# Weights of the projections stored in 4 KB rows, and the one-hots of the gates' second index built on VectorE

## The chip, the core and the metric

One of the eight cores of a Trainium2 chip runs the whole layer; the other cores take no part. The core has TensorE (PE, with its weight loads shown apart as PEld), VectorE (DVE), ScalarE (ACT), GpSimd (POOL) and SyncE (SP), each with a queue of instructions that it takes in order, and 16 DMA engines that all queues share. The metric is the device time of one execution in microseconds, and a measurement of this kernel can tell about 1% from no change.

## The reference, cut to what matters

```python
proj = einsum('bsd,de->bse', rms_norm(x, norm_mix), w_in)      # 1024 tokens, 1024 -> 2560 channels
o_sb = stick_breaking_attention(q, k, v)                        # 8 heads of 64
o_rg = rg_lru(conv(x_rg)) * gelu(g_rg)                          # 512 channels
x = x + concat(rms_norm(o_sb), rms_norm(o_rg)) @ w_out          # 1024 -> 1024
h = rms_norm(x)
# PEER: 8 heads, two halves of 128 keys each, 16384 experts of one neuron
q = einsum('td,dhk->thk', h, w_query)                           # 1024 -> 2048
s = einsum('thpk,hpnk->thpn', q, sub_keys)
top 16 of each half; top 16 of their 256 sums: idx = i1 * 128 + i2, g = softmax
act = gelu(einsum('td,thkd->thk', h, expert_u[idx]))            # 128 slots for each token
x = x + einsum('thk,thkd->td', g * act, expert_v[idx])
```

All arithmetic is float32, and the two expert tables have 64 MB each.

## The kernel before

The 1024 tokens are 8 tiles of 128. They go through the first half of the layer in five groups: tile 0, tiles 1 and 2, 3 and 4, 5 and 6, and 7. Each group has stages with one letter each: n (norm), i (projections to q, k, v), p and r (the RG-LRU branch), a (attention), o (output projection), q (PEER queries, scores, and the 16 best of each half) and s (the 16 best pairs, their experts and softmax). The weights come in pieces of 512 KB, each 128 columns of a matrix: `columns` loads them for w_in (`wi`, `wx`, `wg`) and w_q (`wq`), and `out_proj` loads `wo`. In memory the matrices lie as in the reference, so that a piece of 128 columns is 1024 runs of 512 bytes (2 KB for `wo`). Four buffers hold `wi`, `wx` and `wg`, three hold `wo` and `wq`.

The expert part is done in two ways. Tiles 0, 1, 2 and 7 are **gathered**: for each of their 4 x 128 = 512 slots, POOL issues an indirect DMA that fetches 128 rows of expert_u (512 KB, one row for each token) and later one of expert_v. DVE takes the dot product with `h2` (`u`, line 663) and adds the weighted rows into `y` (line 678). Tiles 3 to 6 are **dense**: for every block e of 128 experts, all 512 tokens are multiplied with the block's expert_u (`s`), passed through gelu (`ga`), weighted with the gate of each token and expert, and multiplied with the block's expert_v (`acc`, `rot`). The products are float32 in three passes of split operands (`uh`, `ul`, `vh`, `vl`, `wh`, `wl`).

The gates of a dense tile come from `gates`. Expert i1 * 128 + i2 has its gate at row i2, column i1 of a 128 x 128 matrix for each token, which is a product over the 128 slots of two matrices: `oa`, the one-hots of i1, and `ob`, the one-hots of i2 times the gate. Four tokens make a group, and a tile has 32 groups, so there are 128 in all. For `ob`, PE first writes i2 - i for every slot, token and column i into PSUM: `less` (line 602) multiplies the transposed i2 with a widened identity, and line 603 adds -i. DVE then compares with zero and multiplies with the gate in one instruction (line 620). `oa` is made on ACT (lines 608 and 609) or on DVE (line 611), by the table `OZS`. PE multiplies `ob` and `oa` into `pg` (line 623), ACT copies that to `gs` (line 624), and a DMA writes each block of 32 tokens to `gd` in DRAM. The dense experts read `gd` back as `gt`, four expert blocks at a time, and line 719 multiplies `ga` with it: the first `ga` can start only when all gates have been written.

The order of the instructions on each queue is not that of the code. `ORDER` gives each stage a priority, and the framework sets the order of every queue when the program is built, from its own model of how long things take:

```python
with tile.TileContext(nc, schedule_with_timeline_sim=True) as tc:
```

Two constants set how the gathered slots are spread. The first `FREE` = 27 blocks of 8 slots (216 slots) may go ahead of the dense experts. Each of the other 296 slots waits for its turn, which is a value that ACT copies from the weights `wh` of a dense block (line 726), so that they keep step with the 128 blocks:

```python
if (k * P + PH) // n_turn == e:
    nc.scalar.activation(turn[:, k:k + 1], wh[:, 0:1].bitcast(F32), AF.Copy)
```

So the program has a mixed part up to the first `ga`, a dense part of 128 blocks in which gathers run beside the products, and an end in which the last gathered slots and the additions of the outputs remain. What is called a slot done below is one `y` instruction on DVE.

Of the kernel before, what the change touches and what calls it, by code (L numbers as in the profile page):

```python
# [46 lines left out]
# the order of priority of the stages of the groups, of the gates of a tile (g), of blocks of gathers (x)  # L47
# [10 lines left out]
def layer(ctx, tc, x, w_in, w_out, w_q, vecs, rga, rgx, skT, eu, ev, euT, out,  # L58
# [14 lines left out]
    # the banks that the last stages do not use are apart: the dense experts start in them  # L73
# [8 lines left out]
    # gate matrices of the dense tokens: gd[j, block of TB tokens, i, token], for expert i * 128 + j  # L82
# [36 lines left out]
    # means over 512 channels, over the channels of a head  # L119
# [6 lines left out]
    # heads 2 c and 2 c + 1 of 8 to chunk c of channels  # L126
# [10 lines left out]
    nob = cp.tile([1, P], BF16, name="nob")  # L137
    nc.vector.tensor_scalar(nob, ioi[0:1, :], -1.0, None, op0=OP.mult)
    ones_b = cp.tile([1, P], BF16, name="ones_b")
    nc.vector.memset(ones_b, 1.0)  # L140
    # rank16[k, s] = k
# [6 lines left out]
    # softplus(-lam) = max(-lam, 0) + ln(1 + exp(-|lam|))  # L148
# [21 lines left out]
    def mm(dst, a, b, first=True, last=True):  # L170
        """dst += sum over k of a[k].T @ b[k]: float32, or pairs of float32r parts"""
# [13 lines left out]
    def columns(pool, tag, w, c0, name, bufs):  # L185
# [10 lines left out]
    def rstd_of(dst, mean):  # L196
        """1 / sqrt(mean + eps)"""
# [25 lines left out]
    # sums of pairs in rows of 8: what no pair takes stays out of reach  # L223
# [3 lines left out]
    # the sums and the normalised rows of the gathered tiles  # L227
# [3 lines left out]
    def norm_in(g):  # L231
# [7 lines left out]
        # x -> h^T  # L239
# [5 lines left out]
    def in_proj(g):  # L245
# [6 lines left out]
        # q, k, v; q stays without its rstd, which the scores take  # L252
        rqk = keep.tile([P, 3, n, 8], F32, tag="rq", name="rq", bufs=2)
        G[g]["rq"] = rqk[:, 1:3]
        for dst, c1, gain, nm in ((kT[:, :, t0:t0 + T], 4, 1, "pk"), (qT, 0, 0, "pq")):
            for c in range(4):
                raw = columns(pj, "wraw", w_in, (c1 + c) * P, "wi", WI)
# [22 lines left out]
        for c in range(4):  # L280
            raw = columns(pj, "wraw", w_in, 1024 + c * P, "wi", WI)
# [6 lines left out]
    def rg_proj(g):  # L288
        """channels on partitions"""
# [4 lines left out]
        for e in range(4):  # L294
            wx = columns(pj, "wraw", w_in, 1536 + e * P, "wx", WI)
            wg = columns(pj, "wraw", w_in, 2048 + e * P, "wg", WI)
# [15 lines left out]
    def rg_lru(g):  # L312
# [16 lines left out]
        # 1 - a^2 = (1 + a^2) tanh(-log a)  # L329
# [9 lines left out]
        # the rstd of each token, to all channels  # L339
# [16 lines left out]
    def attention(g):  # L356
        act, qT, rq = (G[g][nm] for nm in ("act", "qT", "rq"))
        for i, tl in enumerate(groups[g]):
# [3 lines left out]
            # heads that share a bank of scores, from one half of the partitions  # L362
            hp = max(1, 512 // N)
            for h0 in {1: range(8), 2: (0, 1, 4, 5), 4: (0, 1)}[hp]:
                po = bank("po", "po", 1)
                right = None
                for c0 in range((N - 1) // 512 * 512, -1, -512):
# [17 lines left out]
                    for s in range(hp):  # L385
                        # om[k] = product of om from k on; the last position of all is masked in every row
# [7 lines left out]
                    if c0:  # L394
                        # the product over this whole chunk
# [17 lines left out]
    def out_proj(g):  # L413
# [35 lines left out]
    def queries(g, heads=range(8)):  # L449
        """PEER queries, scores, the 16 best of each half"""  # L450
# [392 lines left out]
```

## Time and profile before

| what | value |
| --- | --- |
| median of 3 runs | 2909.61 us |
| lowest and highest | 2885.03 and 2914.87 us |
| span of the profiled execution | 2904.6 us (its own time beside the span is not listed) |
| busy share of the span | PE 92%, DVE 83%, ACT 46%, POOL 48% |
| DMA | 888.90 MB, 306 GB/s over the span |

The profile shows one execution. The span is the time from its first to its last instruction; the median of the runs lies 5.0 us above it. The busy time of an engine is the sum of its instructions, and matmuls are pipelined, so that PE counts as busy a little longer than it is. A granted clock of 1.00 is TensorE's full 2.4 GHz.

### The profile page before, as it was taken

What the parts mean: (1) busy time and instruction counts of PE and PEld (TensorE: products, weight loads), DVE (VectorE), ACT (ScalarE), POOL (GpSimd) and SP (SyncE); (2) the same over time, 40 slices, a digit from 0 to 9 for tenths busy, and PEclk for the clock granted to TensorE, in tenths of its full rate; (3) what the DMA queues carried; (4) which work ended last, traced back from release to release, by engine and by line L of the source; (5) the groups of instructions that cost most, each with busy time, mean ns of one, the idle gap of its engine ahead of it and who ended that gap; (6) DMA issues with size and microseconds to landing.
All of it is one profiled execution on the core that took longest, in us unless ns stands there. A gap on an engine that the chain in (4) does not pass through costs nothing.

```text
span 2904.6 us, 38604 instructions
## 1 busy us (share of the span) xinstructions
PE 2659.0 (92%) x12664; PEld 2103.5 (72%) x12664; DVE 2404.2 (83%) x5235; ACT 1336.3 (46%) x3255; POOL 1401.6 (48%) x1110
## 2 busy tenths in 40 slices
PE   7896989888997988988789999999999999999994
PEld 7685757766784576666567888888888888888883
DVE  2168779987998879998879979888888889888898
ACT  4426434434355633986834443434444434444432
POOL 0134654354444443323446546555655556555565
PEclk9997999898997889978889999999999999999997
DMA  8596888899977688987999989999999999999998
GB/s 235 162 325 223 289 308 297 268 308 297 293 237 250 226 288 291 327 285 268 334 321 360 347 315 365 328 338 352 323 347 339 333 325 352 334 348 329 335 331 307
DMA packets 470168, 888.90 MB, mean 306 GB/s; under 512 B 27600, under 2 KB 286672, under 8 KB 467920
## 3 DMA queue, kind: packets, MB, share of 16 engines
q0 software_dynamic: 147456, 536.94, 52.2%
q1 hardware_dynamic: 322512, 349.51, 36.1%
q8 instruction: 100, 1.64, 0.2%
q14 instruction: 100, 0.82, 0.1%
HBM read 841.25 MB, written 45.09 MB: 305 GB/s over the span
## 4 chain that ended last, share of the span: by engine, by line
PE 61%; DMA 13%; DVE 11%; issue 6%; ACT 5%; POOL 3%; SPq 0%; POOLq 0%; DVEq 0%; ACTq 0%
PE s L177 23%; PE acc L177 16%; PE rot L177 5%; DMA v<-in_ev_dram,idx 4%; DMA u<-in_eu_dram,idx 3%; DMA wq<-in_w_q_dram 3%; PE pqq L194 2%; PE pg L623 2%; DVE u L663 2%; PE pxg L194 2%; DVE y L678 2%; PE pv L285 2%; PE po L429 1%; PE z L377 1%; POOL v L652 1%
## 5 line engine op out<-in xcount | busy, mean ns | idle before, releaser
L652 POOL DMA_INDIRECT u<-in_eu_dram,idx x512 | 666.7, 1302 | 702.0 <-DVE y L678 340.5
L652 POOL DMA_INDIRECT v<-in_ev_dram,idx x512 | 665.2, 1299 | 609.7 <-DVE y L678 193.0
L678 DVE SCALAR_TENSOR_TENSOR y<-v,dots,y 128x1024 f32<-128x1024 f32 x512 | 654.9, 1279 | 48.4 <-DMA v<-in_ev_dram,idx 43.4
L663 DVE SCALAR_TENSOR_TENSOR u<-u,h 128x1024 f32<-128x1024 f32 x512 | 617.3, 1218 | 63.3 <-DMA u<-in_eu_dram,idx 62.0
L177 PE MATMUL s<-h2T,uh 128*128 128x512 f32 x2048 | 505.2, 396 | 0.0
L177 PEld LDWEIGHTS s<-h2T,uh 128*128 128x128 f32 x2048 | 385.5, 188 | 93.4 <-issue 0.2
L177 PE MATMUL acc<-vh,wl 128*128 128x512 f32 x768 | 300.1, 391 | 21.3 <-DVE wl L183 21.2
L177 PE MATMUL acc<-vl,wh 128*128 128x512 f32 x768 | 300.5, 391 | 0.1
L177 PE MATMUL acc<-vh,wh 128*128 128x512 f32 x768 | 299.9, 391 | 0.0
L177 PE MATMUL s<-h2T,ul 128*128 128x512 f32 x1024 | 264.3, 398 | 2.0 <-DVE ul L183 2.0
L194 PE MATMUL pqq<-act,wq 128*128 128x256 f32 (+1 forms) x1280 | 243.1, 347 | 10.9 <-DMA wq<-in_w_q_dram 10.9
L194 PEld LDWEIGHTS pqq<-act,wq 128*128 128x128 f32 x1280 | 208.7, 196 | 36.1 <-DMA wq<-in_w_q_dram 13.1
L177 PEld LDWEIGHTS s<-h2T,ul 128*128 128x128 f32 x1024 | 193.2, 189 | 49.3 <-DVE ul L183 1.8
L182 ACT ACTIVATE vh<-vr 128x512 fp32r<-128x512 f32 x256 | 159.1, 627 | 149.1 <-PE acc L177 70.1
L183 DVE TENSOR_TENSOR vl<-vr,vh 128x512 fp32r<-128x512 f32 x256 | 174.4, 687 | 50.6 <-ACT vh L182 47.1
L623 PE MATMUL pg<-oa,ob 128*128 128x128 f32 x1024 | 166.1, 315 | 37.8 <-DVE ob L620 26.6
L623 PEld LDWEIGHTS pg<-oa,ob 128*128 128x128 f32 x1024 | 148.2, 221 | 64.4 <-issue 22.4
L177 PEld LDWEIGHTS acc<-vh,wl 128*128 128x128 f32 x768 | 144.8, 189 | 53.6 <-issue 21.0
L717 ACT ACTIVATE ga<-s 128x512 f32<-128x512 f32 x128 | 76.4, 597 | 222.9 <-PE s L177 221.3
L624 ACT ACTIVATE gs<-pg 128x512 f32<-128x512 f32 x128 | 136.2, 1080 | 86.2 <-PE pg L623 69.4
L183 DVE TENSOR_TENSOR ul<-ur,uh 128x1024 fp32r<-128x1024 f32 x128 | 156.4, 1222 | 14.3 <-ACT uh L182 13.5
L177 PEld LDWEIGHTS acc<-vl,wh 128*128 128x128 f32 x768 | 144.9, 189 | 31.8 <-DVE vl L183 0.5
(238 smaller groups left out, 4445.1 us busy)
## 6 DMA issues: line engine op xcount, KB each, us to landing
vr<-in_ev_dram SPq DMA_DIRECT2D x128, 512.0 KB
ur<-in_euT_dram SPq DMA_DIRECT2D x128, 512.0 KB
wq<-in_w_q_dram SPq DMA_DIRECT2D x80, 512.0 KB
gd<-gs SPq DMA_DIRECT2D x16, 2048.0 KB
gt<-gd SPq DMA_DIRECT2D x32, 1024.0 KB
wi<-in_w_in_dram SPq DMA_DIRECT2D x60, 512.0 KB
wo<-in_w_out_dram SPq DMA_DIRECT2D x40, 512.0 KB
wx<-in_w_in_dram SPq DMA_DIRECT2D x20, 512.0 KB
```

The source lines that it names most:

```text
L177: nc.tensor.matmul(dst, a[k][u], b[k][v], start=first and i == 0, stop=last and i == len(terms) * n - 1)
L182: nc.scalar.activation(hi, src, AF.Copy)
L183: nc.vector.tensor_tensor(lo, src, hi.bitcast(F32), op=OP.subtract)
L194: nc.tensor.matmul(dst, w[:, k, :], act[:, k, :], start=k == 0, stop=k == DK - 1)
L285: nc.tensor.matmul(pv[:, i * P:(i + 1) * P], act[:, k, i * P:(i + 1) * P], raw[:, k, :], start=k == 0, stop=k == DK - 1)
L377: nc.tensor.matmul(zz, qT[pp, h // 2, qs], kT[pp, h // 2, c0:c0 + w], start=True, stop=not diag)
L623: nc.tensor.matmul(pg[:, t * P:(t + 1) * P], ob[:, t, :], oa[:, t, :], start=True, stop=True)
L624: nc.scalar.activation(gs[:, :, t4:t4 + 4].rearrange("p i t -> p t i"), pg.rearrange("p (t i) -> p t i", t=4), AF.Copy)
L652: nc.gpsimd.indirect_dma_start(out=t, out_offset=None, in_=table, in_offset=bass.IndirectOffsetOnAxis(ap=idx[:, s:s + 1], axis=0))
L663: nc.vector.scalar_tensor_tensor(u, u, 1.0, h2, op0=OP.mult, op1=OP.mult, accum_out=dots[:, s:s + 1])
L678: nc.vector.scalar_tensor_tensor(y, v, dots[:, s:s + 1], y, op0=OP.mult, op1=OP.add)
L717: nc.scalar.activation(ga, sp[:, :ND], AF.Gelu_apprx_tanh)
```

## The change

The host stores w_in and w_q as pieces of 128 columns, [piece, partition, chunk, column], and w_out as pieces [half, quarter, partition, chunk, column], so that each partition's share of a piece is one run of 4 KB. The sub-keys are stored by head, their runs of 1 KB stay. The buffers, the sizes of the pieces and their number are as before.

In `gates`, i1 and i2 are both transposed into `tr`, and `less` and its constants go: 256 matmuls on PE with their weight loads, and the 128 instructions of line 620, give way to 512 `tensor_scalar` instructions on DVE, one for each token. Each compares the row 0 to 127 (`iof`) with the token's i2 and multiplies with its gate, both given as one value for each partition. `tr` gets a second buffer.

```diff
     def columns(pool, tag, w, c, name, bufs):
         raw = pool.tile([P, DK, P], F32, tag=tag, name=name, bufs=bufs)
-        nc.sync.dma_start(raw, w[:, c0:c0 + P].rearrange("(k p) n -> p k n", p=P))
+        nc.sync.dma_start(raw, w[c])
         return raw
...
-                nc.sync.dma_start(raw, w_out[q * 256:(q + 1) * 256, c * 512:(c + 1) * 512].rearrange("(k p) n -> p k n", p=P))
+                nc.sync.dma_start(raw, w_out[c, q])
...
-        tr = gp.tile([P, 3, P], F32, tag="tr", name="tr", bufs=1)
+        tr = gp.tile([P, 3, P], F32, tag="tr", name="tr", bufs=2)
         pb = bank("in", "pb", 2, BF16)
-        nc.tensor.transpose(pb[:, 0:P], i1, ident_b)
-        nc.scalar.activation(tr[:, 0], pb[:, 0:P], AF.Copy)
+        for s in range(2):
+            nc.tensor.transpose(pb[:, s * P:(s + 1) * P], ij[:, s].rearrange("p h k -> p (h k)"), ident_b)
+        nc.scalar.activation(tr[:, 0:2], pb[:, 0:2 * P].rearrange("p (s t) -> p s t", s=2), AF.Copy)
         pt = b_in("pt")
         nc.tensor.transpose(pt[:, 0:P], gtl.rearrange("p h k -> p (h k)"), ident)
-        nc.scalar.activation(tr[:, 1], pt[:, 0:P], AF.Copy)
-        nc.scalar.activation(tr[:, 2], pt[:, 0:P], AF.Copy, scale=-1.0)
+        nc.scalar.activation(tr[:, 2], pt[:, 0:P], AF.Copy)
...
-                def less(ix):
-                    """index - i, for every i, for the slots of 4 tokens"""
-                    d = bank("in" if i < GS else "z", "d", 2).rearrange("p (t i) -> p t i", t=4)
-                    nc.tensor.matmul(d, ix, ident_b[:, tk:tk + 4, None].to_broadcast(sh), start=True, stop=False)
-                    nc.tensor.matmul(d, ones_b, nob[:, None, :].to_broadcast([1, 4, P]), start=False, stop=True)
-                    return d
...
-                    nc.vector.scalar_tensor_tensor(ob, less(i2), 0.0, tr[:, 1, tk:tk + 4, None].to_broadcast(sh), op0=OP.is_equal, op1=OP.mult)
+                for t in range(4):
+                    nc.vector.tensor_scalar(ob[:, t], iof, tr[:, 1, tk + t:tk + t + 1], tr[:, 2, tk + t:tk + t + 1], op0=OP.is_equal, op1=OP.mult)
```

Since the framework orders the queues anew, the change also moves instructions. Up to the first gates the order is the same on every engine. Three places of the new order follow; a row is one instruction, with xN for N equal ones in a row, and the line numbers are those of each kernel.

On PE, in the gates of tiles 5 and 6, before: each group of four tokens has its two difference products and their weight loads ahead of the four products `pg`.

```order
L602 LDWEIGHTS ij
L602 MATMUL d<-ident_b,ij 128x512
L603 LDWEIGHTS ones_b
L603 MATMUL d<-nob,ones_b 128x512
L623 MATMUL pg<-oa,ob 128x128 x4
L602 LDWEIGHTS ij
L602 MATMUL d<-ident_b,ij 128x512
L603 LDWEIGHTS ones_b
L603 MATMUL d<-nob,ones_b 128x512
L623 MATMUL pg<-oa,ob 128x128 x8
```

The same place on PE in the changed kernel: the queries `pqq` and scores `sc` of tile 7 are all ahead, and the 128 products of tile 5 and those of tile 6 stand alone.

```order
L189 MATMUL pqq<-act,wq 128x128 x16
L465 MATMUL sc<-skh,qq 128x128 x2
L580 LDWEIGHTS ij
L580 MATMUL pb<-ident_b,ij 128x128
L603 MATMUL pg<-oa,ob 128x128 x128
L580 LDWEIGHTS ij
L580 MATMUL pb<-ident_b,ij 128x128
L583 MATMUL pt<-ident,g 128x128
L172 MATMUL s<-h2T_9750,ul 128x512 x8
```

On DVE, ahead of the first `ga` of the dense experts, before: the last `ob` of the gates is four rows and six slots away from it (`u` and `y` are gathered slots, `vl` a split of expert_v).

```order
L620 SCALAR_TENSOR_TENSOR ob<-d,tr 128x512
L678 SCALAR_TENSOR_TENSOR y<-v,dots,y 128x1024 x4
L183 TENSOR_TENSOR vl<-vr,vh 128x512 x2
L678 SCALAR_TENSOR_TENSOR y<-v,dots,y 128x1024
L183 TENSOR_TENSOR vl<-vr,vh 128x512 x2
L678 SCALAR_TENSOR_TENSOR y<-v,dots,y 128x1024
L663 SCALAR_TENSOR_TENSOR u,dots<-u,h_20539 128x1024 x2
L719 TENSOR_TENSOR ga<-ga,gt 128x512 x2
```

The same place on DVE in the changed kernel: the end of the selection for tile 7 (`oh`, `ijw`, `idx`) now lies there too. Counted over the whole queue, 184 slots are done ahead of the first `ga`, where it was 208, and 473 ahead of the last one, where it was 498.

```order
L658 SCALAR_TENSOR_TENSOR y<-v,dots,y 128x1024
L545 TENSOR_TENSOR oh<-oh 128x4x32
L658 SCALAR_TENSOR_TENSOR y<-v,dots,y 128x1024
L546 TENSOR_TENSOR ijw<-oh 128x64
L643 SCALAR_TENSOR_TENSOR u,dots<-u,h_20535 128x1024
L554 SCALAR_TENSOR_TENSOR idx<-ijw 128x128
L643 SCALAR_TENSOR_TENSOR u,dots<-u,h_20535 128x1024
L178 TENSOR_TENSOR vl<-vr,vh 128x512 x2
L643 SCALAR_TENSOR_TENSOR u,dots<-u,h_20535 128x1024
L178 TENSOR_TENSOR vl<-vr,vh 128x512 x2
L643 SCALAR_TENSOR_TENSOR u,dots<-u,h_20535 128x1024
L699 TENSOR_TENSOR ga<-ga,gt 128x512 x2
```

At the end of DVE's queue, before, the last gathered slot and the last additions of the dense outputs (`xo`) stand together.

```order
L663 SCALAR_TENSOR_TENSOR u,dots<-u,h_22845 128x1024
L666 TENSOR_TENSOR dots<-dots,g 128x1
L678 SCALAR_TENSOR_TENSOR y<-v,dots,y 128x1024
L759 TENSOR_TENSOR xo<-xo,yr_1_9778 128x512
L759 TENSOR_TENSOR xo<-xo,yr_1_9779 128x512
L839 UNCONDITIONAL_BRANCH
```

In the changed kernel, behind the last `xo`, 21 slots follow; these are the first of them. From the last `ga` to the end of the queue there are 39 slots, where there were 14.

```order
L739 TENSOR_TENSOR xo<-xo,yr_1_9775 128x512
L646 TENSOR_TENSOR dots<-dots,g 128x1 x2
L658 SCALAR_TENSOR_TENSOR y<-v,dots,y 128x1024 x2
L643 SCALAR_TENSOR_TENSOR u,dots<-u,h_22841 128x1024 x2
L646 TENSOR_TENSOR dots<-dots,g 128x1 x2
L658 SCALAR_TENSOR_TENSOR y<-v,dots,y 128x1024 x2
```

## Rows read from the trace of the kernel before

**Rows 1.** The table by stretch: PE, PEld, DVE, ACT, POOL busy; clock; DMA share; GB/s.

```profile
0.00:250.00 250.00, 195.12 (x1242) 172.29 (x1242) 100.13 (x413) 109.08 (x264) 49.56 (x59) 0.91 0.76 234
250.00:935.00 685.00, 615.78 (x3073) 473.01 (x3073) 596.66 (x1684) 303.61 (x694) 336.13 (x286) 0.91 0.85 282
935.00:1441.00 506.00, 447.95 (x2291) 318.54 (x2291) 443.95 (x1218) 343.74 (x711) 178.60 (x158) 0.86 0.84 287
1441.00:1462.00 21.00, 1.86 (x15) 1.48 (x13) 13.01 (x16) 5.07 (x7) 8.98 (x8) 0.59 0.96 326
1462.00:2855.00 1393.00, 1389.49 (x6012) 1131.59 (x6013) 1210.83 (x1846) 568.02 (x1554) 800.58 (x582) 1.00 0.94 337
2855.00:2905.00 50.00, 8.77 (x38) 6.62 (x36) 39.58 (x63) 6.79 (x28) 27.80 (x20) 0.63 0.86 316
30.00:70.00 40.00, 38.43 (x311) 36.00 (x311) 11.26 (x33) 16.59 (x57) 1.92 (x2) 0.98 0.66 188
2860.00:2880.00 20.00, 4.12 (x19) 3.07 (x17) 19.39 (x32) 3.71 (x15) 16.34 (x13) 0.71 0.98 364
```

**Rows 2.** Groups by line and form from 935 to 1441: busy, mean ns, idle before.

```profile
L624 ACT ACTIVATE gs<-pg 128x512 f32<-128x512 f32 x126 | 134.2, 1080 | 85.9 <-PE pg L623 69.1 <-DMA gd<-gs 10.3 <-issue 6.3
...
L678 DVE SCALAR_TENSOR_TENSOR y<-v,dots,y 128x1024 f32<-128x1024 f32 x74 | 94.4, 1276 | 4.5 <-DMA v<-in_ev_dram,idx 4.4
L663 DVE SCALAR_TENSOR_TENSOR u<-u,h 128x1024 f32<-128x1024 f32 x73 | 88.3, 1217 | 19.0 <-DMA u<-in_eu_dram,idx 19.0
L620 DVE SCALAR_TENSOR_TENSOR ob<-d,tr 128x512 f32<-128x512 f32 x128 | 86.9, 682 | 14.2 <-PE d L603 13.3 <-issue 0.7
...
L602 PE MATMUL d<-ident_b,ij 128*128 128x512 bf16 x128 | 55.5, 433 | 4.1 <-DVE ob L620 2.9 <-ACT om L383 1.2
L603 PE MATMUL d<-nob,ones_b 1*128 1x512 bf16 x128 | 55.3, 432 | 0.0
```

**Rows 3.** What DVE waited for, 935 to 1441: us, times, longest.

```profile
DVE u L663 <- DMA u<-in_eu_dram,idx: 19.0, 10, 5.3
DVE ob L620 <- PE d L603: 13.3, 13, 5.2
DVE oa L611 <- PE pg L623: 9.7, 9, 2.8
```

**Rows 4.** DVE's instructions in order of time, 1302 to 1303: start, us.

```profile
1302.58 0.22 DVE L522 TENSOR_SCALAR ri<-bi 128x128 int32<-128x128 int32 x1
1302.71 0.22 DVE L523 TENSOR_SCALAR ri<-bi 128x128 int32<-128x128 int32 x1
```

**Rows 5.** The table by stretch, two bursts of gates.

```profile
1160.00:1260.00 100.00, 90.46 (x601) 69.17 (x599) 93.50 (x322) 97.32 (x230) 29.65 (x28) 0.92 0.95 325
1385.00:1441.00 56.00, 53.09 (x302) 34.66 (x301) 49.20 (x78) 51.97 (x105) 20.42 (x20) 0.92 0.91 336
```

**Rows 6.** What PE waited for, 0 to 935.

```profile
PE po L429 <- DMA wo<-in_w_out_dram: 11.1, 4, 5.0
...
PE pqq L194 <- DMA wq<-in_w_q_dram: 5.6, 3, 4.0
```

**Rows 7.** The chain that ended last, single pieces: start, us, what.

```profile
170.37 12.86 DMA wq<-in_w_q_dram
...
842.25 7.01 DMA wx<-in_w_in_dram
...
1113.57 15.92 DMA wq<-in_w_q_dram
...
1457.75 13.60 DMA vr<-in_ev_dram
```

**Rows 8.** DVE's instructions, last ga and last slot.

```profile
2854.63 0.69 DVE L719 TENSOR_TENSOR ga<-ga,gt 128x512 f32<-128x512 f32 x1
...
2897.25 1.28 DVE L678 SCALAR_TENSOR_TENSOR y<-v,dots,y 128x1024 f32<-128x1024 f32 x1
```

**Rows 9.** The gathers of line 652: ns, min/median/max.

```profile
L652 POOL DMA_INDIRECT u<-in_eu_dram,idx x512: 935/1147/3415, 159.0 to 2887.4; - x171
```

More of the change, by code (lines that the diff above doesn't have):

```diff
@@ L136, in layer @@
     nc.gpsimd.iota(ioi, pattern=[[1, P]], base=0, channel_multiplier=0)
[L137 to L140, printed above, removed]
     rank16 = cp.tile([P, 16, 16], BF16, name="rank16")
@@ L183, in split, with columns @@
         nc.vector.tensor_tensor(lo, src, hi.bitcast(F32), op=OP.subtract)
-    def columns(pool, tag, w, c0, name, bufs):
+    def columns(pool, tag, w, c, name, bufs):
         raw = pool.tile([P, DK, P], F32, tag=tag, name=name, bufs=bufs)
-        nc.sync.dma_start(raw, w[:, c0:c0 + P].rearrange("(k p) n -> p k n", p=P))
+        nc.sync.dma_start(raw, w[c])
         return raw
@@ L256, in in_proj @@
             for c in range(4):
-                raw = columns(pj, "wraw", w_in, (c1 + c) * P, "wi", WI)
+                raw = columns(pj, "wraw", w_in, c1 + c, "wi", WI)
                 pq = b_in(nm)
@@ L280, in in_proj @@
         for c in range(4):
-            raw = columns(pj, "wraw", w_in, 1024 + c * P, "wi", WI)
+            raw = columns(pj, "wraw", w_in, 8 + c, "wi", WI)
             pv = b_in("pv")
@@ L294, in rg_proj @@
         for e in range(4):
-            wx = columns(pj, "wraw", w_in, 1536 + e * P, "wx", WI)
-            wg = columns(pj, "wraw", w_in, 2048 + e * P, "wg", WI)
+            wx = columns(pj, "wraw", w_in, 12 + e, "wx", WI)
+            wg = columns(pj, "wraw", w_in, 16 + e, "wg", WI)
             pxg = b_in("pxg")
@@ L460, in queries @@
             for s in range(2):
-                raw = columns(wk, "wo", w_q, (2 * h + s) * P, "wq", WO)
+                raw = columns(wk, "wo", w_q, 2 * h + s, "wq", WO)
                 chans_mm(pq[:, s * 256:s * 256 + T], raw, act)
@@ L465, in queries @@
             skh = wk.tile([P, 2, P], F32, tag="skh", name="skh", bufs=2)
-            nc.sync.dma_start(skh, skT[:, 2 * h:2 * h + 2, :])
+            nc.sync.dma_start(skh, skT[h])
             sc = b_op("sc").rearrange("p (s t) -> p s t", s=2)
@@ L580, in gates @@
         _, gtl, ij = topk_out[tl]
[L581 to L583 removed]
+        tr = gp.tile([P, 3, P], F32, tag="tr", name="tr", bufs=2)
         pb = bank("in", "pb", 2, BF16)
[L585 to L586 removed]
+        for s in range(2):
+            nc.tensor.transpose(pb[:, s * P:(s + 1) * P], ij[:, s].rearrange("p h k -> p (h k)"), ident_b)
+        nc.scalar.activation(tr[:, 0:2], pb[:, 0:2 * P].rearrange("p (s t) -> p s t", s=2), AF.Copy)
         pt = b_in("pt")
         nc.tensor.transpose(pt[:, 0:P], gtl.rearrange("p h k -> p (h k)"), ident)
[L589 to L590 removed]
+        nc.scalar.activation(tr[:, 2], pt[:, 0:P], AF.Copy)
+        sh = [P, 4, P]
         for b in range(P // TB):
@@ L612, in gates @@
                 ob = work(gp, "ob", 512, OB).rearrange("p (t i) -> p t i", t=4)
-                if t4 // 4 % OBS[i] == OBS[i] - 1:
-                    nc.scalar.activation(ob, less(i2), AF.Abs)
-                    for t in range(4):
-                        g = tr[:, 1, tk + t:tk + t + 1]
-                        nc.scalar.activation(ob[:, t], ob[:, t], AF.Relu, bias=g, scale=tr[:, 2, tk + t:tk + t + 1])
-                else:
-                    nc.vector.scalar_tensor_tensor(ob, less(i2), 0.0, tr[:, 1, tk:tk + 4, None].to_broadcast(sh), op0=OP.is_equal, op1=OP.mult)
+                for t in range(4):
+                    nc.vector.tensor_scalar(ob[:, t], iof, tr[:, 1, tk + t:tk + t + 1], tr[:, 2, tk + t:tk + t + 1], op0=OP.is_equal, op1=OP.mult)
                 pg = b_in("pg")
@@ L816, in blocks, with columns @@
         return w.reshape(4, 2, 64, 64).transpose(1, 2, 0, 3).reshape(P, 4, 64)
+    def columns(w):
+        return w.reshape(DK, P, -1, P).transpose(2, 1, 0, 3)
     return {
-        "x": a["x"][0], "w_in": a["w_in"][0], "w_out": a["w_out"][0], "w_q": a["peer_w_query"][0].reshape(D, 2048),
+        "x": a["x"][0], "w_in": columns(a["w_in"][0]), "w_q": columns(a["peer_w_query"][0].reshape(D, 2048)),
+        "w_out": a["w_out"][0].reshape(4, 2, P, 2, 512).transpose(3, 0, 2, 1, 4),
         "vecs": vecs, "rga": blocks(a["rg_w_a"][0]), "rgx": blocks(a["rg_w_x"][0]),
-        "skT": a["peer_sub_keys"][0].reshape(16, P, P).transpose(2, 0, 1),
+        "skT": a["peer_sub_keys"][0].reshape(8, 2, P, P).transpose(0, 3, 1, 2),
         "eu": a["peer_u"][0], "ev": a["peer_v"][0],
```

3 lines of the change are left out of this document (removed).

## The prediction, made before the changed kernel ran

> **What bounds the kernel now.** I read the table by stretch first, cut where the work changes: the start, the middle, the stretch with the gates of the dense tiles, the 21 us before the first `ga`, the dense experts, the end [rows 1]. In the dense part PE is busy for 1389.5 of 1393 us at clock 1.00: nothing but PE's products limits it. No instruction of PE there changes, and the order puts 498 - 208 = 290 slots beside it before and 473 - 184 = 289 after. I count this part as unchanged. So the time can move in two places only: how early the first `ga` starts, and how much is left after the last.
>
> From 935 to 1441 the reader is to see that no engine stands out: PE is busy for 448, DVE for 444, ACT for 344 of 506 us, and DMA has a share of .84. The same view of the two bursts of gates shows the third candidate: ACT is busy for 97.3 of 100 and for 52.0 of 56 us [rows 5]. The groups by line say what each does [rows 2], the waits of DVE whom it waits for [rows 3], and the chain that ended last has pieces in which a weight's transfer is all that runs [rows 7]. At the end, 14 slots lie between the last `ga` at 2854.63 and the last `y` at 2897.25 [rows 8].
>
> **The change part by part.**
>
> *The differences leave PE.* 256 matmuls of .43 us go, 55.5 + 55.3 = 111 us of PE [rows 2], all in the 506 us. That is the most that the stage could win from PE alone. What it wins depends on DVE and ACT, which are as full.
>
> *The one-hots on DVE.* Neighbours on DVE overlap: two instructions of .22 us on 128x128 start .13 us apart [rows 4]. I take .08 off each duration accordingly. Then the 128 `ob` that go give back 128 x .60 = 77 us. The 512 that come have the shape of [rows 4], but read two values for each partition, which no row of this size does. The lower bound of their pitch is .13 (67 us in all). For the upper I take .25, the .22 of the row with no overlap and some more (128 us). The only hint on the cost of such an operand is that `y`, which has one, takes 1276 ns, and `u`, which has none, 1217 [rows 2]: .06. I choose .13 + .06, rounded up to .20: 102 us, or 25 us more than what goes, between -10 and +51.
>
> *What the order moves.* Up to the last `ob`, DVE now has 26 `y` and 24 `u` fewer, with 26 x 1.20 + 24 x 1.14 = 59 us, and some selection for tile 7 that I put at 8 us. DVE's work to that point changes by +25 - 59 - 8 = -42 us (-77 to -16). DVE's waits for PE in the stage, 13.3 for `d` and 9.7 for `pg` [rows 3], go with the differences: `ob` no longer needs PE, and PE reaches `pg` sooner. That makes -65. But in the two bursts, 156 us, ACT copies `pg` at 1080 ns a group without a pause [rows 2, 5], and neither half of the change relieves it. I let the gain count in the other 350 of 506 us: -45. Against it stands that DVE now has some 25 us of instructions between its last `ob` and the first `ga`, where it had 12. Half of that fits into the 21 us in which the gates travel to DRAM and back [rows 1], in which DVE had 8 us free. I add 4. The stage: -41, between 0 (ACT sets it all) and -100 (-77 and all 23 us of waits).
>
> *Rows of 4 KB.* In the stretch 30 to 70, in which weights alone travel, the DMA engines moved 188 GB/s at a share of .66, or 285 at a full one. In 2860 to 2880, in which gathers of 4 KB rows alone travel, it is 364 at .98, or 371 [rows 1]. So a piece of 512 KB goes from 1.84 to 1.41 us of all 16 engines, and the 180 pieces (36 of `w_in` and `w_q` for each of five groups) from 331 to 254: 77 us of DMA time. Little of it is on the path. PE waited 11.1 us for `wo` and 5.6 for `wq` up to 935 [rows 6], and the chain has several pieces such as 12.86, 7.01 and 15.92 [rows 7]. The share of the DMA engines stays under .86 until 1441, with gathers taking the rest. I take -20: the 16.7 us of waits and a few of the chain's pieces. The bounds are 0 (the queue is hidden anyway) and -45 (a quarter more off each of some twelve such pieces and the waits besides).
>
> The Trainium skill, "DMA: Bandwidth & Descriptors", section "Specifications", puts the smallest transfer at line rate at 512 bytes. By it rows of 512 bytes lose nothing to rows of 4 KB, this part would be worth 0, and the sum below would be +36. The trace here speaks against it: 285 to 371 GB/s at a full share [rows 1].
>
> *The two transposes and the second buffer of* `tr`. One more transpose of 128 columns for each tile, 4 in all, each under the .43 us of a product of 512 [rows 2], in the midst of other products of PE: nothing. If this cover went, it would be 2 us.
>
> *The end.* The order leaves 39 slots after the last `ga` in place of 14, with their `u` and `v` gathers. The 14 took 2897.25 + 1.28 - 2854.63 = 43.9 us, or 3.1 us each [rows 8]. A slot's two gathers of 512 KB take 2.83 us at 371 GB/s, so DMA sets this pace, and nothing in the change makes it faster. 25 x 3.1 = +77 us (25 x 2.83 = 71 at the least). The 50 fewer instructions ahead of the first `ga` are therefore not a gift: they come back at the end, where no product covers them.
>
> *The sum.* -20 - 41 + 77 = +16. The profiled span of 2904.6 becomes 2920.6 and its first `ga` moves from 1461.7 to about 1401. The median lies 5.0 above the span: 2909.6 + 16 = **2926**. The break-even is a first `ga` that is 77 us earlier, at 1385.
>
> **The rivals.**
>
> *A: PE sets the stage (faster).* If what looks like ACT's and DVE's fullness is only PE's pace handed on, the 111 us come off whole. For it: DVE waited 23 us for PE and ACT 69.1 us for `pg` [rows 2, 3]; PE, DVE and DMA are all relieved at once, since 26 MB of gathers leave the stage too. Against it: ACT at 97% in the burst [rows 5]. It gives -111 - 20 + 77 = -54, so 2856; with the layout at its bound of -45, 2831.
>
> *B: DVE sets the stage (slower).* The waits for PE turn into waits for ACT or for `u` (19.0 us, the longest of DVE's waits already [rows 3]), and the new instructions come at the upper pitch. With a pitch p the stage is 512 p - 77 - 59 - 8 + 4, with +77 at the end and nothing from the layout: 512 p - 63. At .25 that is +65: 2975. It is past 1%, or 29 us, from p = .18 on, and with the layout's -20 from .22 on. For it: DVE is at 93.5 of 100 in the first burst [rows 5]. Against it: the shape's pitch in the trace is .13 [rows 4].
>
> *C: the layout does not do what it says.* A transfer of expert_v with rows of 4 KB also took 13.60 us at the end of the chain [rows 7], as long as the `wq` of 512-byte rows: a piece lands when the gathers ahead of it let it. Then weights land no sooner, -41 + 77 = +36: 2946.
>
> *D: the one-hots hold up the gathers.* POOL issues every gather, in 935 to 3415 ns, with a median of 1147 [rows 9]. If it is delayed by what DVE does at the time, bursts of four short instructions lie in its way where one stood, and I double DVE's 19.0 us of waits for `u` [rows 3]: +16 + 19 = +35, so 2945. Against it: POOL is idle for 327 of the 506 us [rows 1].
>
> The Trainium skill, "SBUF — State Buffer", section "SBUF: two separate sides", has a rule for this: a DVE operation in a 2-port mode locks GpSimd out of the port by which it writes its descriptors. By it each `tensor_scalar`, if it ran in such a mode, would be such a lock; the spread from 935 to 3415 ns would fit, but no row here ties a long gather to an instruction of DVE.
>
> **How the numbers follow.** The forecast has .37, A .27, B .20, C .10, D .06. About 1% is what a measurement of this kernel can tell from no change, so the classes are divided at 2881 and 2939. A gives .23 to faster and the lower part of the forecast's own spread (a stage of -100 instead of -41 gives 2867) .06. B gives .18 to slower, C and D .10, the forecast's upper part (a stage near 0 gives 2967) .04. That makes .29, .39 and .32. For the range, I leave out half of B's cases above 2975 and a good third of A's below 2840. The forecast's own range is 2867 to 2967.
>
> **What the changed profile would show.** The forecast holds if the dense part takes about 1393 us with PE at 100%, 39 slots follow the last `ga` at about 3.1 us each, the first `ga` stands near 1401, the new `ob` have starts .20 us apart, and ACT is still full in the bursts. A is right if the first `ga` is before 1350 and ACT's copies come closer than before. B is right if DVE is at 95% in the stage and `ob` stand .22 us apart or more. C is right if `wq` transfers last as long as before, and D if the waits for `u` grow and POOL's gathers take longer. The prediction is wrong altogether if the dense part is not bound by PE alone: DMA there is at .94, and if the gathers fall behind, PE waits for `ur` or `gt`. It is wrong too if the end goes at another pace than 3.1 us a slot.

## The result, and the profile after

The changed kernel takes 2946.4 us (median; 2934.2 to 2947.4) against 2906.9 us for the kernel before, measured beside it: a ratio of 1.014, with a 95% interval from 1.009 to 1.019. It is 39.5 us slower, where +16 was forecast and the forecast range reached to 2975.

The table by stretch shows where this is, cut where the changed kernel's work changes. Its columns are those of [rows 1].

```profile
0.00:250.00 250.00, 201.36 (x1278) 177.96 (x1279) 108.15 (x430) 111.79 (x270) 50.48 (x61) 0.91 0.67 237
250.00:935.00 685.00, 613.94 (x3049) 468.92 (x3049) 592.33 (x1676) 304.47 (x696) 335.70 (x285) 0.91 0.81 282
935.00:1402.00 467.00, 356.53 (x2041) 302.07 (x2039) 439.01 (x1512) 339.82 (x697) 132.03 (x111) 0.87 0.73 261
1402.00:1423.00 21.00, 0.00 (x0) 0.00 (x0) 8.76 (x15) 2.19 (x4) 8.52 (x8) 0.50 0.97 335
1423.00:2812.00 1389.00, 1384.34 (x5995) 1128.22 (x5996) 1205.98 (x1826) 561.08 (x1510) 787.14 (x575) 1.00 0.94 335
2812.00:2862.00 50.00, 12.24 (x54) 9.78 (x53) 40.99 (x67) 7.69 (x33) 35.52 (x29) 0.67 0.96 343
2862.00:2944.50 82.50, 0.00 (x0) 0.00 (x0) 62.06 (x96) 9.12 (x45) 56.75 (x43) 0.50 0.86 308
30.00:70.00 40.00, 38.28 (x316) 35.60 (x314) 11.26 (x33) 18.32 (x60) 1.92 (x2) 1.00 0.60 199
```

The dense part is as before, 1389 us with PE full. Behind it stands a row that the kernel before does not have: 82.5 us in which PE does nothing at all, and DVE, POOL and the DMA engines work off slots. DMA is the fullest of them, with a share of .86. In the stage of the gates, DVE is busy for 439 of 467 us (94%), where it was 444 of 506 [rows 1]; PE fell from 88% to 76%. The granted clock of this stage is .87, where it was .86, so it explains none of the difference.

The group of the one-hots, by line and form from 935 to 1402, with the copies of `pg` and the slots' `y` (columns as in [rows 2]), and then DVE's instructions in order of time in the midst of the gates (as in [rows 4]):

```profile
L600 DVE TENSOR_SCALAR ob<-iof,tr 128x128 f32<-128x128 f32 x509 | 140.9, 355 | 1.3 <-PE pg L603 1.3
L604 ACT ACTIVATE gs<-pg 128x512 f32<-128x512 f32 x128 | 132.9, 1063 | 26.6 <-PE pg L603 16.1 <-DMA gd<-gs 10.4
L658 DVE SCALAR_TENSOR_TENSOR y<-v,dots,y 128x1024 f32<-128x1024 f32 x56 | 71.6, 1278 | 5.6 <-DMA v<-in_ev_dram,idx 5.4
```

```profile
1370.12 2.15 DVE L600 TENSOR_SCALAR ob<-iof,tr 128x128 f32<-128x128 f32 x8
1372.17 0.70 DVE L542 TENSOR_TENSOR oh<-ab,rank 128x1024 bf16<-128x1024 bf16 x1
```

Eight `tensor_scalar` take 2.05 us from the first start to the next instruction's, so they stand .26 us apart. DVE's busy time for `ob` is 140.9 us, against 86.9 [rows 2]: +54 (509 of the 512 are in this view). What it waited for in the same stretch (us, times, longest), against [rows 3]:

```profile
DVE u L643 <- DMA u<-in_eu_dram,idx: 6.4, 4, 2.3
DVE y L658 <- DMA v<-in_ev_dram,idx: 5.4, 3, 3.5
DVE oa L597 <- PE pg L603: 5.2, 3, 2.3
```

The waits of `ob` for PE are gone but for 1.3 us, and those of `u` are a third of what they were. Now PE waits for ACT, by the same view:

```profile
PE pg L603 <- ACT gs L604: 42.4, 44, 4.6
```

Last, the way from the last gates to the first `ga`, in the chain that ended last (start, us, what):

```profile
1395.46 8.85 DMA u<-in_eu_dram,idx
...
1405.57 0.21 DVE idx L554
...
1405.90 17.95 DMA gt<-gd
1423.87 0.70 DVE ga L699
```

The last copy of the gates on ACT (`gs`) starts at 1391.3 and the first `ga` at 1423.9, 32.6 us later; before it was 1443.1 and 1461.7, 18.6 us. The load of `gt` is not issued when the gates have landed, at 1403.4, but when the selection of tile 7 has written its `idx`, which DVE's new order puts behind the last `ob`. (In the code, the pool of `gt` opens on the side of memory where the pool of the selection was closed, so it may take over its memory; the trace shows the order and not the reason.) Ahead of that `idx`, DVE waits for a `u` that is landing. The `gt` then takes 18 us until it lets the first `ga` start, beside seven gathers that are issued from 1405.8 to 1414.3, six of them of `u`; before, it took at most 8 (issued at 1453.8).

The account of the two profiled executions, from these starts:

| piece | before | after | difference | forecast |
| --- | --- | --- | --- | --- |
| start to first `ga` | 1461.7 | 1423.9 | -37.8 | -61 |
| first to last `ga` | 1392.9 | 1387.7 | -5.2 | 0 |
| last `ga` to the end | 50.0 | 132.9 | +82.9 | +77 |
| span | 2904.6 | 2944.5 | +39.9 | +16 |

Each column is one execution. The dense part, whose products are the same in all kernels below, took between 1384 and 1401 us in their profiled executions, so a few us in such an account can be chance.

### The profile page after: what moved, and what is told of

It reads as the page before. It is cut to its first block, busy times and chain, and to the rows that moved or that the text cites. A ratio compares the mean times of both kernels' runs of the same rounds, so it can differ in the third digit from the quotient of the medians.

```text
span 2944.5 us, 38471 instructions
## 1 busy us (share of the span) xinstructions
PE 2568.4 (87%) x12412; PEld 2087.0 (71%) x12412; DVE 2457.3 (83%) x5617; ACT 1336.2 (45%) x3253; POOL 1406.1 (48%) x1110
## 4 chain that ended last, share of the span: by engine, by line
PE 54%; DMA 14%; DVE 13%; ACT 7%; issue 7%; POOL 4%; SPq 0%; POOLq 0%; DVEq 0%; ACTq 0%
PE s L172 21%; PE acc L172 16%; DMA v<-in_ev_dram,idx 8%; PE rot L172 5%; DMA u<-in_eu_dram,idx 3%; DVE u L643 3%; PE pxg L189 2%; POOL v L632 2%; PE pqq L189 2%; DVE ob L600 2%; POOL u L632 2%; ACT gs L604 2%; DVE y L658 2%; PE pk L189 1%; PE po L401 1%
## 5 line engine op out<-in xcount | busy, mean ns | idle before, releaser
L632 POOL DMA_INDIRECT v<-in_ev_dram,idx x512 | 673.3, 1315 | 696.6 <-DVE y L658 272.5
L178 DVE TENSOR_TENSOR vl<-vr,vh 128x512 fp32r<-128x512 f32 x256 | 174.6, 687 | 54.7 <-ACT vh L177 54.2
L603 PE MATMUL pg<-oa,ob 128*128 128x128 f32 x1024 | 162.2, 318 | 62.0 <-ACT gs L604 42.4
L172 PEld LDWEIGHTS acc<-vh,wh 128*128 128x128 f32 x768 | 144.6, 188 | 30.6
```

The costliest lines, as they stand in the source:

```text
L172: nc.tensor.matmul(dst, a[k][u], b[k][v], start=first and i == 0, stop=last and i == len(terms) * n - 1)
L603: nc.tensor.matmul(pg[:, t * P:(t + 1) * P], ob[:, t, :], oa[:, t, :], start=True, stop=True)
L632: nc.gpsimd.indirect_dma_start(out=t, out_offset=None, in_=table, in_offset=bass.IndirectOffsetOnAxis(ap=idx[:, s:s + 1], axis=0))
```

## The experiments

Theory 1 was formed from this account: DVE's dearer one-hots push gathered slots behind the last `ga`, where a slot costs more than ahead of the first one; PE's relief is real, and DVE spends it. The rivals are named in the expectations. Where the slots stand is set when the program is built, by the framework's own model; each order below was counted from the queue. The diffs show the lines that matter.

**The layout alone.** The kernel before with the rows of 4 KB.

```diff
-        nc.sync.dma_start(raw, w[:, c0:c0 + P].rearrange("(k p) n -> p k n", p=P))
+        nc.sync.dma_start(raw, w[c])
```

> The kernel before with the 4 KB rows alone; the one-hots stay as before. The order of DVE's queue is that of before, 208 slots ahead of the first ga and 14 behind the last, so only the transfers differ. Theory 1 (the weights are hidden behind the queue): the scores of the third group stood only 2 us earlier in the changed kernel, so this is worth 0 to -8 us, the first ga at 1453 to 1462. Rival 2 (the layout is worth what I predicted and the one-hots are dearer than they look): -20 us or more, first ga at 1442 or before.

It took 2891.5 us, a ratio of .995 (.9926 to .9975) to the kernel before: 14 us faster by the ratio. The first `ga` starts at 1450.4, 11 us earlier, and the end is as before, 50.5 us. Both guesses missed, the truth being between them. The waits of PE for weights show where it comes from; first the kernel before and then the layout alone, 0 to 1400, all rows of this kind:

```profile
PE po L429 <- DMA wo<-in_w_out_dram: 13.0, 5, 5.0
PE pqq L194 <- DMA wq<-in_w_q_dram: 10.9, 7, 4.0
PE pq L194 <- DMA wi<-in_w_in_dram: 4.8, 1, 4.8
PE pxg L194 <- DMA wx<-in_w_in_dram: 1.1, 1, 1.1
```

```profile
PE po L429 <- DMA wo<-in_w_out_dram: 4.2, 3, 3.6
PE pq L194 <- DMA wi<-in_w_in_dram: 2.6, 1, 2.6
```

That is 29.8 - 6.8 = 23 us less of PE's waits, of which the first `ga` gained 11.

**The one-hots alone.** The changed kernel with the rows of 512 bytes, which is the diff above the other way round.

> The changed kernel with the rows of 512 bytes; the one-hots on DVE stay. The order has 184 slots ahead of the first ga and 39 behind the last, as in the changed kernel. Theory 1: 40 to 48 us slower than before, about the whole difference, with the first ga near 1428 and some 133 us after the last. Rival 2: +60 us, with the first ga at 1444 or later.

2956.6 us, a ratio of 1.0153 (1.0109 to 1.0197). Theory 1 holds: first `ga` at 1426.5, 134.1 us after the last one begins. The loss comes with the one-hots alone, and with the order that they bring. The layout on top of them takes 2.6 us off the first `ga` in the profiles, though it takes PE's waits for weights up to 1400 from 32.3 us to 15.1; the intervals of the two ratios are too wide to say more of it.

**The slots' order without the one-hots.** The kernel before, with fewer slots let ahead.

```diff
-FREE = 27
+FREE = 23
```

> The kernel before with FREE at 23: nothing changes but that 184 slots may go ahead of the dense experts. The order then has 184 slots ahead of the first ga and 38 behind the last, as the changed kernel has. Theory 1 (24 slots moved behind the last ga cost 3.3 us each there and give back only a part ahead): the end grows by about 79 us, from 50 to 129. If DVE set the stage of before, the first ga comes 24 x 2.4 = 58 us earlier and the total is +20 us; if PE set it, the first ga hardly moves and the total is +60 us or more. Rival 3 (the order of the slots is worth nothing, their time is only moved): within 10 us of before.

2955.0 us, a ratio of 1.0144 (1.0101 to 1.0187). So the order of the slots by itself costs as much as the whole change did, with every instruction of before in place. The end grew from 50.0 to 129.4 us, 3.3 for each of the 24 slots, and the first `ga` came only 28 us earlier, 1.2 for each. That lies between the two guesses, which fits a stage that was set by PE and DVE in turn. Two views bear this out. With 24 slots fewer ahead, DVE waited longer for PE: the first two rows, from 935 to 1441, come to 44 us, where the same two were 23 [rows 3]. And PE waited for `ob` in the kernel before, as the row of its products `pg` from 935 to 1443 shows (third row). The profiled execution was the slowest of its kernel, 10 us above the median.

```profile
DVE ob L620 <- PE d L603: 23.3, 22, 4.8
DVE oa L611 <- PE pg L623: 20.5, 23, 3.9
L623 PE MATMUL pg<-oa,ob 128*128 128x128 f32 x1024 | 166.1, 315 | 37.8 <-DVE ob L620 26.6 <-ACT h2T L182 3.4 <-ACT gs L624 2.7
```

**PE's relief without DVE's price.** The kernel before; `dfix` is a tile of zeros that stands for the difference.

```diff
-                    nc.tensor.matmul(d, ix, ident_b[:, tk:tk + 4, None].to_broadcast(sh), start=True, stop=False)
-                    nc.tensor.matmul(d, ones_b, nob[:, None, :].to_broadcast([1, 4, P]), start=False, stop=True)
-                    return d
+                    return dfix.rearrange("p (t i) -> p t i", t=4)
```

> The kernel before with the 256 difference products of PE left out: ob is made from a tile of zeros instead of i2 - i, with the same instruction on DVE, so the gates are not those of the reference. 111 us of PE go and DVE's count stays. The order has 192 slots ahead of the first ga and 30 behind the last. The end grows by 16 x 3.3 = 53 us in any case. Theory 1 (PE's relief is real, DVE's dearer one-hots spend it): the first ga 80 to 100 us earlier than 1462, the total -25 to -45 us. Rival 4 (DVE or ACT set the stage, PE's relief is worth nothing by itself): the first ga only 16 x 2.4 = 38 us earlier, the total +15 us.

2893.4 us, a ratio of .9954 (.9926 to .9981), 13 us faster: the sign of theory 1 with half its size, and rival 4 falls. The last `gs` starts at 1357.0, 86 us earlier, but the first `ga` at 1394.8, 67 us earlier, where theory 1 had 80 to 100: here too the selection of tile 7 stands behind the last `ob` (its `idx` at 1377.5), and `gt` comes late. The end takes 103.5 us from the last `ga` at 2783.6, 53.5 more than before, as expected. The views of `gs` and `ga` in this kernel, then in the one-hots alone (ns; first and last start in us):

```profile
L623 ACT ACTIVATE gs<-pg x128: 1012/1078/1197, 945.9 to 1357.0; 128x512 f32<-128x512 f32 x128
L718 DVE TENSOR_TENSOR ga<-ga,gt x128: 676/692/736, 1394.8 to 2783.6; 128x512 f32<-128x512 f32 x128
```

```profile
L604 ACT ACTIVATE gs<-pg x128: 999/1062/1286, 948.3 to 1399.8; 128x512 f32<-128x512 f32 x128
L699 DVE TENSOR_TENSOR ga<-ga,gt x128: 678/690/708, 1426.5 to 2821.0; 128x512 f32<-128x512 f32 x128
```

Against this kernel, the one-hots alone are +43 us at the last `gs` and +32 at the first `ga`, with 8 slots fewer ahead: that is what they cost DVE.

The order of this kernel also corrects theory 1. It has 30 slots behind the last `ga` with DVE's instructions as before, and the changed kernel has 39, where it was 14. So 16 of the 25 slots move with PE's relief alone, and only the other 9 come with the one-hots. That the framework finds less time for slots in a shorter stage would fit; its model was not looked into.

**All `oa` on ACT.** The changed kernel with

```diff
-OZS = (2, 1, 2, 2)
+OZS = (1, 1, 1, 1)
```

> The changed kernel with OZS at 1 for all four tiles: the 48 oa that DVE makes, .69 us each, go to ACT (about 1.9 us each there). DVE loses 33 us, ACT gains 91. The order has 200 slots ahead of the first ga and 20 behind the last (184 and 39 in the changed kernel). Theory 1 (slots are what DVE's fullness pushes behind the last ga; 3.3 us each there): the end shrinks from 133 to about 70 us; the first ga comes later by what 16 slots cost ahead, 1.2 to 2.4 us each, less the relief of 33: between 14 us earlier and 5 later. Total 40 to 60 us faster than the changed kernel, 2890 to 2905. Rival 5 (ACT takes over as the bound, 340 + 91 = 431 of 467 us): the first ga 30 us later or more, the total about 2915.

2935.3 us, a ratio of 1.0097 to the kernel before (1.0064 to 1.0130). The median is 11 us below that of the changed kernel, but the intervals of the two ratios overlap; it lies above both guesses. Each theory had one half. The end shrank to 70.1 us, as theory 1 said, but the first `ga` came at 1466.2, 42 later, as rival 5 said. ACT is full in the last gates (44.6 of 46 us, second row), and something unforeseen came with it, the granted clock of PE. PE's products `pg` in the whole stage are the third row: they wait 21.7 us for `oa` from ACT, where the changed kernel's wait 2.4, and they are busy for 199.8 us, where the changed kernel's are busy for 162.2.

```profile
1350.00:1400.00 50.00, 28.58 (x118) 24.46 (x116) 43.20 (x115) 41.80 (x99) 13.31 (x13) 0.59 0.68 246
1400.00:1446.00 46.00, 35.88 (x144) 31.10 (x144) 33.16 (x85) 44.63 (x103) 21.61 (x18) 0.54 0.77 273
L603 PE MATMUL pg<-oa,ob 128*128 128x128 f32 x1024 | 199.8, 362 | 79.7 <-ACT gs L604 38.8 <-ACT oa L595 21.7 <-DVE ob L600 18.9
```

**One tile's one-hots on DVE.** The changed kernel where `i > 0` (tiles 4 to 6) has the difference products and the single instruction of before, and OZS is (1, 1, 2, 2).

```diff
+                if i > 0:
+                    nc.tensor.matmul(d, ij[:, 1].rearrange("p h k -> p (h k)"), ident_b[:, tk:tk + 4, None].to_broadcast(sh), start=True, stop=False)
+                    nc.tensor.matmul(d, ones_b, nob[:, None, :].to_broadcast([1, 4, P]), start=False, stop=True)
+                    nc.vector.scalar_tensor_tensor(ob, d, 0.0, tr[:, 2, tk:tk + 4, None].to_broadcast(sh), op0=OP.is_equal, op1=OP.mult)
```

> The changed kernel, with its rows of 4 KB, where only tile 3 has its ob from tensor_scalar on DVE; tiles 4 to 6 have the difference products on PE and the single instruction on DVE, as before. OZS is (1, 1, 2, 2), so that the 16 oa of tile 3 that DVE made go to ACT. PE loses 28 us against before, DVE gains 15 and loses 11, ACT gains 30. The order has 208 slots ahead of the first ga and 14 behind the last, as before. Theory 1 (PE's relief counts where DVE does not pay for it with slots): the first ga 5 to 20 us before that of the layout alone (1450), the end 50 us, total 2872 to 2887. Rival 5 (ACT is the bound): no gain over the layout alone, 2891 or above.

2899.4 us, a ratio of .9984 (.9965 to 1.0003): not faster than the layout alone, as rival 5 said. The profiled execution has its first `ga` at 1441.4, 9 us before that of the layout alone, as theory 1 said, but it was the fastest of twelve (2890.5), and the median does not bear the gain out. The order with 14 slots at the end brought the end back to 54.7 us.

**The selection of tile 7 earlier.** The changed kernel with

```diff
-ORDER = "... q4 g4 g5 g6 s4"
+ORDER = "... q4 s4 g4 g5 g6"
```

> The changed kernel with the stage s4, the selection of tile 7, ahead of g4, g5 and g6 in ORDER. DVE's last idx stands 12 instructions behind the last ob, where it stood 27, and the first ga 21 behind it, where it stood 35. Slots: 184 ahead of the first ga as before, 41 behind the last (39). Theory 1 (the load of the first gt waits for that selection, and its gathers then crowd the load): the time from the last gs to the first ga falls from 32.6 to about 20 us, the end grows by 2 x 3.3 us, total 0 to -8 us against the changed kernel. Rival 6 (the time to the first ga is only the way of the gates through DRAM): it stays above 28 us and the total is 5 us slower.

The mechanism is right: `idx` stands at 1386.9, the time from the last `gs` (1383.6) to the first `ga` (1406.2) is 22.6 us in place of 32.6, and the first `ga` is 17.7 us earlier. The total is 2946.3 us, a ratio of 1.0145 (1.0110 to 1.0179), nothing gained: the end took 145.9 us, 13 more, where 2 slots more were to cost 6.6. Where the rest of the 13 comes from was not followed up.

**The price of an operand by partition.** The four instructions of a group in the changed kernel in four forms; `i2` and `g` are the four tokens' columns of `tr`.

```diff
+                nc.vector.tensor_scalar(ob[:, 0], iof, i2[:, 0:1], g[:, 0:1], op0=OP.is_equal, op1=OP.mult)
+                nc.vector.tensor_scalar(ob[:, 1], iof, i2[:, 1:2], None, op0=OP.is_equal)
+                nc.vector.tensor_scalar(ob[:, 2], iof, 2.0, 0.5, op0=OP.is_equal, op1=OP.mult)
+                nc.vector.tensor_scalar(ob[:, 3], iof, 3.0, None, op0=OP.is_equal)
```

> The changed kernel with the four tensor_scalar of a group in four forms: two values by partition (as it is), one value by partition and no product, two constants, one constant. Three of four tokens then have no right one-hots or gates. All write 128x128 float32 from iof. If the two operands by partition made the .277 us (I had taken .13 + .06 a piece), the forms with constants take about .13 to .14 and that with one operand .20. Rival 7 (a float32 instruction of 128 columns costs this much whatever its scalars are): all four within .02 us of each other.

DVE's instructions in order of time in this kernel; line 600 has two such values, 601 one, 602 and 603 none:

```profile
1360.37 0.34 DVE L600 TENSOR_SCALAR ob<-iof,tr 128x128 f32<-128x128 f32 x1
1360.63 0.28 DVE L601 TENSOR_SCALAR ob<-iof,tr 128x128 f32<-128x128 f32 x1
1360.83 0.22 DVE L602 TENSOR_SCALAR ob<-iof 128x128 f32<-128x128 f32 x1
1360.96 0.22 DVE L603 TENSOR_SCALAR ob<-iof 128x128 f32<-128x128 f32 x1
1361.10 0.34 DVE L600 TENSOR_SCALAR ob<-iof,tr 128x128 f32<-128x128 f32 x1
```

The starts are .26, .20, .13 and .14 us apart: .13 for the instruction and .06 to .07 for each value by partition. Rival 7 falls. (The kernel ran once, in 2914.2 us; it has 32 slots behind the last `ga`, and 111.9 us there.)

**More slots ahead, on the layout alone.**

```diff
-FREE = 27
+FREE = 28
-ORDER = "... q4 g4 g5 g6 s4"
+ORDER = "... q4 x28 g4 g5 g6 s4"
```

> The kernel before with the 4 KB rows, FREE at 28 and x28 ahead of g4 in ORDER, which gives the first 28 blocks of slots the priority over the gates of tiles 4 to 6. The order then has 211 slots ahead of the first ga and 11 behind the last (208 and 14 in the layout alone). Theory 1 (a slot behind the last ga costs some 3.3 us, and some 1.2 ahead of the first, as FREE at 23 showed): the end 10 us shorter, the first ga 4 us later, total 2885, or 6 us faster than the layout alone. Rival 8 (the stage of the gates has no room left, a slot ahead costs 2.4 us or more): no faster than the layout alone, 2888 to 2900.

2892.5 us, a ratio of .9972 (.9952 to .9992) to the kernel before: the same as the layout alone. The end is 47.9 us (2.6 less, for 3 slots), the first `ga` at 1460.3 in the profiled execution, 10 us later. Rival 8 stands: here a slot ahead costs some 3 us, where FREE at 23 gave back 1.2.

**Less of DVE in tile 3, on the layout alone.**

```diff
-OZS = (2, 1, 2, 2)
+OZS = (1, 1, 2, 2)
```

> The kernel before with the 4 KB rows and OZS (1, 1, 2, 2): the 16 oa of tile 3 that DVE made, 11 us, go to ACT. The order has 208 slots ahead of the first ga and 15 behind the last. Theory 1 (DVE is what fills the stage, ACT has room at tile 3, before the bursts): the first ga 5 to 10 us earlier than the layout alone (1450), the end 3 us longer, total 2884 to 2889. Rival 5 (ACT is late as soon as it gets more, as when all oa went to it): the first ga later than 1450, the total 2895 or more.

2891.7 us, a ratio of .996 (.9932 to .9988): again the layout alone, between the two guesses. The first `ga` is at 1453.1, later as rival 5 said, and the end takes 57.8 us for 15 slots. It tells nothing apart. No kernel run is faster than the layout alone, at 2891.5 us, half a per cent under the kernel before and 1.9% under the changed kernel (.995 / 1.0141); the last two and the one without difference products are equal to it within the noise.

## Why the prediction was right, and where it was off

The sum by its terms, with the one-hots alone as the step between the kernel before and the changed one (profiled executions, us):

| term | forecast | measured | from |
| --- | --- | --- | --- |
| rows of 4 KB | -20 | -3 | first `ga`, 1426.5 to 1423.9 |
| the stage up to the first `ga` | -41 | -35 | first `ga`, 1461.7 to 1426.5 |
| dense part | 0 | -5 | first to last `ga` |
| the end | +77 | +83 | last `ga` to the end |
| sum | +16 | +40 | |

The sign and the mechanism of the loss were right. Most of the 24 us that the sum is off lies in the layout. The stage came out within 6 us, but by luck: two large errors in it had opposite signs.

**The end.** This was the term that decided, and it held: +82.9 us where +77 were forecast, 3.3 us for a slot where 3.1 were read from [rows 8]. The runs bear it out with every order that they had, by the profiled executions:

| kernel | slots behind the last `ga` | last `ga` to the end, us |
| --- | --- | --- |
| more slots ahead | 11 | 47.9 |
| before | 14 | 50.0 |
| layout alone | 14 | 50.5 |
| one tile's one-hots | 14 | 54.7 |
| less of DVE in tile 3 | 15 | 57.8 |
| all `oa` on ACT | 20 | 70.1 |
| no difference products | 30 | 103.5 |
| four forms | 32 | 111.9 |
| FREE at 23 | 38 | 129.4 |
| changed kernel | 39 | 132.9 |
| one-hots alone | 39 | 134.1 |
| selection earlier | 41 | 145.9 |

**The one-hots on DVE: the step that failed.** I wrote ".13 + .06, rounded up to .20", with one operand by partition, and had said a sentence before that the instruction reads two. With both it is .13 + 2 x .06 = .25, which the changed kernel (.26) and the four forms show. DVE's `ob` grew by 54 us in the stage, where +25 was forecast. My upper bound of +51 was nearly the truth. DVE's work up to the last gates was to shrink by 42 us; it shrank by 12, from 444 us in 506 to 432 in 456:

```profile
935.00:1391.00 456.00, 356.25 (x2041) 302.07 (x2039) 431.92 (x1499) 337.93 (x695) 127.93 (x107) 0.88 0.72 258
```

**PE's relief** was taken too low. I let the stage win DVE's 23 us of waits, and only outside the bursts, because ACT is full in these. By the same row, what DVE stands idle in the stage fell from 62 us to 24, or by 38. Without the difference products the last `gs` came 86 us earlier. The 16 slots fewer are about 19 of these at 1.2 each, or 38 at the 2.4 that one takes of DVE, so the relief is an estimated 48 to 67 us. ACT did not stand in its way: that kernel left ACT's work as it was. I had also misread its fullness as copies of `pg` alone: from 1160 to 1260 the copies took 34 of ACT's 97 us, and most of the rest was `oa` (first three rows). In the changed kernel only 16 copies fall into that stretch, and ACT is busy for 48 us of it (last two rows). Elsewhere it is still full, as for 38 of the 41 us from 1350 to 1391.

```profile
L608 ACT ACTIVATE oa<-iof,tr 128x128 f32<-128x128 f32 x128 | 42.2, 456 | 0.0
L624 ACT ACTIVATE gs<-pg 128x512 f32<-128x512 f32 x31 | 34.6, 1127 | 2.7 <-PE pg L623 2.7
L609 ACT ACTIVATE oa<-oa,ones 128x512 f32<-128x512 f32 x31 | 23.5, 782 | 0.0
L604 ACT ACTIVATE gs<-pg 128x512 f32<-128x512 f32 x16 | 16.4, 1050 | 2.0 <-PE pg L603 2.0
1160.00:1260.00 100.00, 66.79 (x435) 60.55 (x435) 96.79 (x436) 48.20 (x102) 23.69 (x25) 0.83 0.75 281
```

So two errors, a relief too small and a price too low, mostly cancelled.

**The way from the last gates to the first** `ga` was put at +4 us. It grew by 14. The part that I had not seen is that the load of `gt` waits for the selection of tile 7, and that its gathers then go beside it; moving that selection ahead took 10 of the 14 away. The stage as a whole is -35 with the one-hots alone, where -41 was forecast.

**The layout** was forecast at -20. It is worth 14 us by the ratio of the layout alone, but some 3 in the changed kernel, by the first `ga` and by the two ratios alike (1.0153 and 1.0141, with wide intervals), so as a term of this sum it was the one most off. PE waited 29.8 us for weights up to 1400 and 6.8 with the long rows, and 32.3 and 15.1 with the one-hots on DVE. Rows of 4 KB move 199 GB/s at a share of .60 in the stretch from 30 to 70, an estimated 332 at a full one, where I had taken 371 from the gathers. The Trainium skill, "DMA: Bandwidth & Descriptors", section "Specifications", puts the smallest transfer at line rate at 512 bytes; the runs here disagree, with 285 GB/s by the same estimate against 332 and a gain that can be measured.

**The rivals.** A (PE sets the stage) is right that PE's relief is real, but its 111 us are more than the 86 by which the last `gs` moved even without DVE's price. B (DVE sets the stage at the upper pitch) names the mechanism best: DVE is 94% busy, at a pitch of .26. Its price of +65 is too high: the three waits of [rows 3] fell from 42.0 us to 12.9 (6.4 for `u`, 5.2 for `oa`, 1.3 for `ob`). With .26 in its formula and these 29 us off, the stage comes to -36, and -35 was measured. C and D forecast the time that was measured, 2946 and 2945, and their mechanisms are wrong. For C, PE's waits for weights do shrink; but its price, nothing from the layout, was nearer than mine in the changed kernel. For D, gathers are issued as before, as the row of POOL's gathers of `u` shows against [rows 9], and DVE's waits for `u` fell.

```profile
L632 POOL DMA_INDIRECT u<-in_eu_dram,idx x512: 932/1143/3416, 155.5 to 2930.7; - x171
```

**What stays open.** Why the layout gives 11 us of first `ga` to the kernel before and 3 to the one with one-hots on DVE was not tried. That DVE has less room there would fit. Nor was the changed kernel tried with the slots in the order of before, 14 behind the last `ga`; the kernel with one tile's one-hots comes nearest to it. That DMA sets the pace of the end is argued from its share (.96 and .86 in the rows from 2812 on), and no run changed it there.

## What to carry to other kernels

Work that a new order puts behind a stage is part of the price of the change, whether the stage became shorter or an engine in it fuller: count, in the new order, what lies behind the last instruction of the part that bounds the kernel, and price it at the pace of the end. An engine that is busy all the time in a burst may be so because work of several kinds falls together there; ask which of it the stage waits for. Count every operand of a short instruction: here each value by partition adds half of what the instruction costs without.

## What the runs showed of the hardware

A `tensor_scalar` on 128x128 float32 had a pitch of .13 us with constants, .20 with one value by partition and .26 with two.

PE's granted clock differed between two similar stages. With all `oa` on ACT it was .59 from 1350 to 1400 and .54 from 1400 to 1446, close to the lower of its two levels (.50 is 1.2 GHz), with PE busy for 29 of 50 and 36 of 46 us; from 1325 to 1350, before it fell, it was 1.00, with PE busy for 24 of 25 us, and from 1275 to 1325 it had been .57 with PE busy for 34 of 50. A `pg` product took 362 ns in the mean over the stage, in place of 318 in the changed kernel (.89 from 1350 to 1391, busy for 28 of 41 us). The 44 ns on 1024 products are 45 us of PE, about the 42 us by which the first `ga` came late, and PE's waits ahead of them grew by 18 us (62.0 to 79.7), chiefly for `oa`; whether the clock or ACT held it back was not told apart.
